# Moving the opening of attention in between the last gate blocks of the projections

## The chip, the core and the metric

The kernel runs on one core of a Trainium2 chip. The metric is the device time of one execution in microseconds. Three runs of the kernel before gave 1424.99 us as median, between 1424.39 and 1425.21.

## What is computed

One decoder layer for 2048 tokens of width 1024, all in float32. A normalised input is projected once; the columns of the projection feed two groups of heads and their gates.

```python
h = rms_norm(x, ln_g)
proj = h @ w_in
q_lat, kv_lat, k_rope, g_mla, hq, hf, hi, g_hg = split(proj)
y_mla = mla_group(q_lat, kv_lat, k_rope, ...) * silu(g_mla)   # 8 heads, causal softmax attention
y_hg  = hgrn2_group(hq, hf, hi, ...) * silu(g_hg)             # 4 heads, gated linear recurrence
x = x + concat(y_mla, y_hg) @ w_out
out = rms_norm(x, final_norm_g)
```

In the attention group the queries and keys come from normalised latents of 256 and 128 columns: `q = q_lat_n @ w_q_b`, `k, v = kv_lat_n @ w_kv_b`, with a rotary part beside them.

## The kernel before

Every product is made of three fp32r matmuls (`mm3`, lines 67 to 70): high by high, high by low, low by high. "Split" means that ScalarE writes the rounded high part (`hi`, line 702) and VectorE the rest (`lo`, line 703); on the `pool=True` path GpSimd does both (lines 699, 700).

The program has three stages. The first (to line 653) makes the projections and the recurrence, 1024 tokens at a time, and writes the latents, the rotary tables and the gates to DRAM (`latq_d`, `latkv_d`, `kpe_d`, `cs_d`, `gate_d`). Its last step is `gates(1, hB)`, line 652: one load of weights and eight blocks of 128 tokens. A block is 24 matmuls of 328 columns into one PSUM bank of the tag `mm`, which has three banks; ScalarE empties it with a SiLU (line 338), and SyncE's queue stores it (line 339). Beside these blocks the last units of the recurrence end: squares (line 513), their sum (515), the scaling (518), a transpose (525), a copy `yt` (527) and its store (528).

The second stage is attention (lines 655 to 1008). It opens with loads of the latents (`load_c`, `load_q`, `load_rope`, `load_cs`, lines 694 to 718) in three slices of the tokens, T0 (0 to 511), T1 (512 to 1023) and T2 (1024 to 2047); with the weights of head 0 (`load_wq`, line 671) and of the keys and values (lines 685 to 692); and with splits of what is loaded. Then come key, query and value of the first 512 tokens (`key`, `query`, `value`), key 1, and the scores of the first two rows of queries (`stage_a(*seq[0], cur)`, line 991). The loop over 64 pairs of head and rows (line 999) merges the scores of the next pair with the transposes and value products of this one. The third stage is the out-projection.

What the first stage holds on the right side of SBUF (pools `raw`, `hg`) is freed by `p1r.close()`, and `lat` of the second stage lies over it; `wk`, `big` and `wk2` lie over the left side after `p1.close()`. A pool that reuses memory waits for all that used it: the first load of attention (line 687) waits for the last store of `yt`.

The lines say in which order work is handed over. A scheduler then sets the order on each engine from its own estimate of the times, and an engine takes its instructions strictly in that order. All loads and stores are issued by SyncE's queue, in its order too.

Of the kernel before, what the change touches and what calls it, by code (L numbers as in the profile page):

```python
# [10 lines left out]
F32 = mybir.dt.float32  # L11
F32R = mybir.dt.float32r
# [7 lines left out]
S = 2048  # L20
D = 1024
# [36 lines left out]
def hybrid_kernel(ctx: ExitStack, tc: tile.TileContext, x, positions, ln_g, w_in, q_a_norm_g, w_q_b,  # L58
# [5 lines left out]
    def f32(ap):  # L64
        return ap.bitcast(F32)
# [583 lines left out]
    U = hg_units(1, 1, raws)  # L649
    merge(U[:16], vv + gg)  # L650
    merge(U[16:], lat_kv(1, hB))
    run(gates(1, hB))
    p1r.close()

# [1 line left out]
    p2 = ExitStack()  # L656
    p2r = ExitStack()
    lat = p2r.enter_context(tc.tile_pool(name="lat", bufs=1, side="right"))
    c_hi = lat.tile([128, S], F32R, name="c_hi")
    c_lo = lat.tile([128, S], F32R, name="c_lo")  # L660
    wv_hi = lat.tile([128, HEADS, VD], F32R, name="wv_hi")
# [9 lines left out]
    def load_wq(h):  # L671
# [9 lines left out]
        A.copy(wqh, wf)  # L681
        G.tensor_tensor(wql, wf, f32(wqh), ALU.subtract)
        return wqh, wql

    G.memset(csT[0:64, 0:1024], 1.0)
    wkv = csT[:, 1024:2048].rearrange("p (h n) -> p h n", h=HEADS)
    DMA.dma_start(wkv, w_kv_b.rearrange("p (h n) -> p h n", h=HEADS))
    V.tensor_scalar(out=wkv, in0=wkv, scalar1=gkv, scalar2=None, op0=ALU.mult)
    A.copy(wk_hi, wkv[:, :, 0:NOPE])
    V.tensor_tensor(wk_lo, wkv[:, :, 0:NOPE], f32(wk_hi), ALU.subtract)  # L690
    A.copy(wv_hi, wkv[:, :, NOPE:128])
    V.tensor_tensor(wv_lo, wkv[:, :, NOPE:128], f32(wv_hi), ALU.subtract)
# [31 lines left out]
    load_c(T0)
    wq0 = load_wq(0)
    load_q(T0)
    load_cs(slice(0, 1024))
    load_rope(T0)
    split_c(T0)
    split_q(T0)  # L730
    split_rope(T0)
    load_c(T1)
    load_q(T1)
    load_rope(T3)
    G.memset(csT[0:64, 1024:2048], 1.0)
    load_cs(T2)
    load_c(T2)
    load_q(T2)
    p1.close()
    wk = p2.enter_context(tc.tile_pool(name="wk", bufs=2, side="left"))  # L740
    big = p2.enter_context(tc.tile_pool(name="big", bufs=1, side="left"))
    wk2 = p2.enter_context(tc.tile_pool(name="wk2", bufs=2, side="left"))
    k_hi1 = big.tile([128, S], F32R, name="k_hi1")
    k_lo1 = big.tile([128, S], F32R, name="k_lo1")
    k_hi, k_lo = (k_hi0, k_hi1), (k_lo0, k_lo1)

    heads = [None] * HEADS

    stash = {}

    def prep(h):
        """Items that make head h's gate, weights, v, k and q (by 512 tokens)."""
        hd = {"k": (k_hi[h % 2], k_lo[h % 2]), "q": [None] * NCHK}
        heads[h] = hd

        def start():
            if h % 2 == 0:
                stash["k"] = wk.tile([64, S], F32, tag="ks", bufs=1, name="ks")
            if h % VG == 0:
                stash["v"] = wk.tile([128, NBLK, VG - 1, VD], F32, tag="vs", bufs=1, name="vs")  # L760
            hd["gate"] = wk2.tile([128, NBLK, VD], F32, tag="gate", name="gate")
            DMA.dma_start(hd["gate"], gate_d[:, h * VD:(h + 1) * VD].rearrange("(b p) n -> p b n", p=128))
            hd["wq"] = wq0 if h == 0 else load_wq(h)
            hd["v"] = wk.tile([128, NBLK, 2, VD], F32R, tag="vp", name="vp")
            if h == 1:
                DMA.dma_start(f32(k_hi1[64:128]), f32(k_hi0[64:128]))
                DMA.dma_start(f32(k_lo1[64:128]), f32(k_lo0[64:128]))

        def value(b4):
# [18 lines left out]

        def key(c):
            kh, kl = hd["k"]  # L790
            ks = stash["k"]
            sl = slice(c * 512, (c + 1) * 512)
            if h % 2 == 0:
                p = bank("b", 1)
                mm3(p, wk_hi[:, h:h + 2].rearrange("p a b -> p (a b)"), wk_lo[:, h:h + 2].rearrange("p a b -> p (a b)"),
                    c_hi[:, sl], c_lo[:, sl], True, True)
                A.copy(kh[0:64, sl], p[0:64])
                V.tensor_tensor(kl[0:64, sl], p[0:64], f32(kh[0:64, sl]), ALU.subtract)
                A.copy(ks[:, sl], p[64:128])
            else:  # L800
                A.copy(kh[0:64, sl], ks[:, sl])
                G.tensor_tensor(kl[0:64, sl], ks[:, sl], f32(kh[0:64, sl]), ALU.subtract)

        def query(c):
            wqh, wql = hd["wq"]
            sl = slice(c * 512, (c + 1) * 512)
            p = mmb()
            for k in range(2):
                mm3(p, wqh[:, k], wql[:, k], q_hi[:, k, sl], q_lo[:, k, sl], k == 0, k == 1)
            qf = wk.tile([128, 512], F32, tag="qf", bufs=1, name="qf")  # L810
            V.tensor_tensor(qf, p, csT[:, sl], ALU.mult)
            qh = wk.tile([128, 512], F32R, tag="qh", bufs=2, name="qh")
            ql = wk.tile([128, 512], F32R, tag="ql", bufs=2, name="ql")
            A.copy(qh, qf)
            (V if h == 0 and c < 2 else G).tensor_tensor(ql, qf, f32(qh), ALU.subtract)  # L815
            hd["q"][c] = (qh, ql)

        its = {"start": start}
        for c in range(NCHK):
            its["k", c] = lambda c=c: key(c)  # L820
            its["v", c] = lambda c=c: value(c)
            its["q", c] = lambda c=c: query(c)
        return its
# [6 lines left out]
        return list(zip(o, w))  # L830

    def stage_a(h, j, ctx_):
        """Scores, negated, with their minimum, then exp: two rows of 128 queries."""
        hd = heads[h]
        items = []
        ctx_["ri"] = [None, None]
# [2 lines left out]
        def score(i, kc):  # L839
# [4 lines left out]
            nk = (qb + 1) * 128  # L844
            chunks = key_chunks(nk)
            if kc == 0:
                ctx_["rows"][i] = wk2.tile([128, S], F32, tag="sn", bufs=4, name="sn")
                ctx_["mx"] = small.tile([128, 5], F32, tag="mx", name="mx")
            sn, mx = ctx_["rows"][i], ctx_["mx"]
            k0, w = chunks[kc]  # L850
# [131 lines left out]
            parts[h][key_]()  # L982
        return do

    for key_ in ("start", ("k", 0), ("q", 0), ("v", 0)):
        parts[0][key_]()
    cur = {}
    av_all = bank("a", 1, (128, 2, 256))
    split_c(T1)
    parts[0]["k", 1]()  # L990
    run(stage_a(*seq[0], cur))
    split_q(T1)
    for i in range(3):
        split_rope(slice(512 + 512 * i, 1024 + 512 * i), pool=True)
    for i in range(2):
        split_c(slice(1024 + 512 * i, 1536 + 512 * i))
    for i in range(2):
        split_q(slice(1024 + 512 * i, 1536 + 512 * i))
# [12 lines left out]
    p3 = ExitStack()  # L1011
    op = p3.enter_context(tc.tile_pool(name="op", bufs=2, side="right"))
    fng = wk.tile([128, D], F32, tag="ks", bufs=1, name="ks")
    DMA.dma_start(fng, final_norm_g.rearrange("(o n) -> o n", o=1).broadcast_to([128, D]))
    for b in range(NBLK):
        c, r0 = b // 4, b * 128
# [67 lines left out]
```

## Time and profile before

| what | value |
|---|---|
| median of three runs | 1424.99 us |
| span of the profiled execution | 1424.0 us |
| TensorE matmul busy | 1395.9 us, 98% of the span |
| VectorE, ScalarE, GpSimd busy | 954.6, 878.6, 464.3 us |
| stretch in question, from the third gate block to full pace in attention | 681.6 to 727.0 us |

The profiled execution's span stands 1.0 us under the median; what lies around the span is in that. The page shows TensorE busy nearly everywhere, with one slice in the middle at 8 tenths instead of 9. That slice holds the passage from projections to attention. In it the time is not TensorE's work but what TensorE waits for, so the rows of that stretch have to be read engine by engine.

### The profile page before, as it was taken

How to read it: one execution, taken by the hardware profiler on the slowest of the kernel's cores; microseconds unless marked ns; L12 is line 12 of the kernel's file. 1: busy time of each engine (PE TensorE's matmuls, PEld its weight loads, DVE VectorE, ACT ScalarE, POOL GpSimd, SP SyncE). 2: the span in 40 equal slices, each digit the busy share in tenths (PEclk: the TensorE clock that was granted, in tenths of full speed). 3: DMA queues.
4: the chain of work that ended last, by engine and by line, in shares of the span. 5: the costliest groups of instructions: out<-in, count | busy, mean ns of one | idle time of the engine just before them, and what ended most of it. 6: DMA issues, size and time to landing. Idle time of an engine off the chain costs nothing.

```text
span 1424.0 us, 25891 instructions
## 1 busy us (share of the span) xinstructions
PE 1395.9 (98%) x9314; PEld 1271.8 (89%) x9314; DVE 954.6 (67%) x2433; ACT 878.6 (62%) x1796; POOL 464.3 (33%) x635
## 2 busy tenths in 40 slices
PE   8999999999999999999989999999999999999998
PEld 7899879989889988999879999999999998888887
DVE  6547855595645746658389889897889888744333
ACT  6565575456672647345387788778877888732232
POOL 3123613083121522227262425233433425411010
PEclk9999999999999999999989999999999999999999
DMA  6211211214221112111640110000010103244342
GB/s 185 75 48 46 75 52 31 70 38 157 64 60 35 45 60 74 45 42 36 165 106 9 28 23 13 22 15 20 15 27 9 25 24 100 79 137 148 133 148 104
DMA packets 96351, 92.10 MB, mean 65 GB/s; under 512 B 31072, under 2 KB 84576, under 8 KB 96096
## 3 DMA queue, kind: packets, MB, share of 16 engines
q1 hardware_dynamic: 96224, 90.46, 21.7%
q8 instruction: 73, 1.20, 0.4%
q14 instruction: 54, 0.44, 0.1%
HBM read 64.22 MB, written 25.17 MB: 63 GB/s over the span
## 4 chain that ended last, share of the span: by engine, by line
PE 86%; DVE 5%; ACT 3%; POOL 2%; DMA 2%; issue 2%; SPq 0%; POOLq 0%; DVEq 0%; ACTq 0%
PE ps_mm L68 14%; PE ps_mm L69 14%; PE ps_mm L70 14%; PE ps_tp L902 8%; PE ps_a L921 5%; PE ps_a L920 4%; PE ps_mm L854 4%; PE ps_mm L855 4%; PE ps_mm L856 4%; PE ps_b L68 2%; PE ps_b L70 2%; PE ps_b L69 2%; PE ps_b L459 1%; PE ps_a L459 1%; POOL dd L441 1%
## 5 line engine op out<-in xcount | busy, mean ns | idle before, releaser
L68 PE MATMUL ps_mm<-w,hh 128*128 128x256 f32 (+3 forms) x896 | 270.2, 302 | 0.0
L69 PE MATMUL ps_mm<-w,hh 128*128 128x256 f32 (+3 forms) x896 | 265.3, 296 | 0.0
L70 PE MATMUL ps_mm<-w,hl 128*128 128x256 f32 (+3 forms) x896 | 264.2, 295 | 0.0
L906 DVE TENSOR_TENSOR pl<-ps_tp,ph 128x512 fp32r<-128x512 f32 (+1 forms) x288 | 184.4, 655 | 32.9 <-ACT ph L905 32.3
L905 ACT CAST ph<-ps_tp 128x512 fp32r<-128x512 f32 (+1 forms) x288 | 154.1, 565 | 61.5 <-PE ps_tp L902 47.3
L68 PEld LDWEIGHTS ps_mm<-w,hh 128*128 128x128 f32 x896 | 171.4, 191 | 1.0 <-ACT kr L234 0.3
L69 PEld LDWEIGHTS ps_mm<-w,hh 128*128 128x128 f32 x896 | 171.2, 191 | 0.4
L70 PEld LDWEIGHTS ps_mm<-w,hl 128*128 128x128 f32 x896 | 170.6, 190 | 0.1
L902 PE MATMUL ps_tp<-ident,sn 128*128 128x128 f32 x1088 | 168.1, 274 | 0.6 <-ACT sn L868 0.5
L868 ACT ACTIVATE sn<-sn,mx 128x128 f32<-128x128 f32 (+15 forms) x128 | 154.6, 1208 | 21.5 <-DVE mx L863 21.0
L920 PE MATMUL ps_a<-ph,vp 128*128 128x256 f32 x576 | 155.5, 290 | 0.0
L921 PE MATMUL ps_a<-pl,vp 128*128 128x256 f32 x576 | 147.3, 289 | 0.3 <-DVE pl L906 0.2
L441 POOL TENSOR_TENSOR dd<-G 128x512 f32<-128x512 f32 x80 | 92.9, 1166 | 144.0 <-DVE qd L454 109.3
L902 PEld LDWEIGHTS ps_tp<-ident,sn 128*128 128x128 f32 x1088 | 126.9, 140 | 8.5 <-ACT sn L868 1.1
L854 PE MATMUL ps_mm<-k_hi,qh 128*128 128x512 f32 (+3 forms) x320 | 131.1, 410 | 0.3 <-DVE sn L859 0.2
L859 DVE TENSOR_SCALAR_CACHE_REDUCE sn<-ps_mm,mx 128x512 f32<-128x512 f32 (+3 forms) x192 | 111.5, 581 | 10.0 <-PE ps_mm L856 8.3
L856 PE MATMUL ps_mm<-k_hi,ql 128*128 128x512 f32 (+3 forms) x320 | 116.7, 365 | 1.2 <-DVE ql L815 1.2
L855 PE MATMUL ps_mm<-k_lo,qh 128*128 128x512 f32 (+3 forms) x320 | 116.4, 364 | 0.0
L203 DVE SCALAR_TENSOR_TENSOR w<-wr,lng,w 128x256 fp32r<-128x256 f32 (+3 forms) x168 | 88.4, 568 | 39.3 <-ACT w L202 39.3
L921 PEld LDWEIGHTS ps_a<-pl,vp 128*128 128x128 f32 x576 | 109.1, 189 | 6.1 <-DVE pl L906 1.4
L920 PEld LDWEIGHTS ps_a<-ph,vp 128*128 128x128 f32 x576 | 109.0, 189 | 5.8 <-ACT ph L905 0.4
L887 POOL TENSOR_SCALAR gp<-gate,ri 128x64 f32<-128x64 f32 x128 | 56.3, 443 | 174.1 <-DVE ri L870 158.4
(275 smaller groups left out, 3355.3 us busy)
## 6 DMA issues: line engine op xcount, KB each, us to landing
wr<-in_w_in SPq DMA_DIRECT2D x68, 256.0 KB
yl<-y_d SPq DMA_DIRECT2D x16, 512.0 KB
vp<-in_x SPq DMA_DIRECT2D x16, 512.0 KB
out<-sn SPq DMA_DIRECT2D x15, 512.0 KB
xt<-in_x SPq DMA_DIRECT2D x8, 512.0 KB
y_d<-yt SPq DMA_DIRECT2D x16, 256.0 KB
gate<-gate_d SPq DMA_DIRECT2D x8, 512.0 KB
y_d<-oa SPq DMA_DIRECT2D x64, 64.0 KB
```

What stands on the lines that cost most here:

```text
L68: PE.matmul(ps, l_hi, r_hi, start=start, stop=False)
L69: PE.matmul(ps, l_hi, r_lo, start=False, stop=False)
L70: PE.matmul(ps, l_lo, r_hi, start=False, stop=stop)
L854: PE.matmul(p[:, :w], qh[:, qs], kh[:, ks], start=True, stop=False)
L855: PE.matmul(p[:, :w], qh[:, qs], kl[:, ks], start=False, stop=False)
L856: PE.matmul(p[:, :w], ql[:, qs], kh[:, ks], start=False, stop=True)
L868: A.activation(sn[:, :nk], sn[:, :nk], AF.Exp, bias=mx[:, kc:kc + 1], scale=-1.0, accum_out=rs)
L902: PE.transpose(tp[:, o:o + 128], prow[i][:, (kb + u) * 128:(kb + u + 1) * 128], ident)
L905: A.copy(ph[:, :w], tp[:, :w])
L906: V.tensor_tensor(pl[:, :w], tp[:, :w], f32(ph[:, :w]), ALU.subtract)
L920: PE.matmul(dst, vv, ph[:, rng], start=st_, stop=False)
L921: PE.matmul(dst, vv, pl[:, rng], start=False, stop=en)
```

## The change

The gates of the last half are no longer run to their end. Only their weights are loaded first (`ga[:1]`); the eight blocks are then merged evenly with a list of items: the loads of attention, its weights, the splits, key 0, query 0, key 1, the scores of the first pair and the remaining splits. Value 0 and the load of the gate stay behind the blocks. Pools of the second stage get `reuse_waits="tile"`, so that a tile waits only for the tiles that it lies over. The scratch of dynamic DMAs is cut to 2048 bytes, and three tags (`ks`, `qf`, `qh`/`ql`) and two small rows (`sn0`) move to a new pool `qk` on the right side.

```diff
-    run(gates(1, hB))
+    ga = gates(1, hB)
+    run(ga[:1])
     p1r.close()
...
+    qk = p2q.enter_context(tc.tile_pool(name="qk", bufs=1, side="right", reuse_waits="tile"))
+    lat = p2r.enter_context(tc.tile_pool(name="lat", bufs=1, side="right", reuse_waits="tile"))
...
-    for key_ in ("start", ("k", 0), ("q", 0), ("v", 0)):
-        parts[0][key_]()
+    def first_loads():
+        load_c(T0)
+        parts[0]["start_k"]()
+        load_q(T0)
+        load_cs(slice(0, 1024))
+        load_rope(T0)
+    def more_loads():
+        load_c(T1)
+        load_q(T1)
+        load_rope(T3)
+        G.memset(csT[0:64, 1024:2048], 1.0)
+        load_cs(T2)
+        load_c(T2)
+        load_q(T2)
+    def opening():
+        split_rope(T0)
+        parts[0]["k", 0]()
+        parts[0]["q", 0]()
+    items = [first_loads, weights, lambda: (split_c(T0), split_q(T0)), more_loads, opening,
+             lambda: split_c(T1), parts[0]["k", 1]] + stage_a(*seq[0], cur)
+    items += [lambda: split_q(T1)] + [lambda i=i: split_rope(thirds(i), pool=True) for i in range(3)]
+    items += [lambda i=i: split_c(thirds(i + 1)) for i in range(2)]
+    items += [lambda i=i: split_q(thirds(i + 1)) for i in range(2)]
+    merge(ga[1:], items)
+    p1.close()
...
+    parts[0]["start"]()
+    parts[0]["v", 0]()
-    nc = bacc.Bacc("TRN2", target_bir_lowering=False, num_devices=1)
+    nc = bacc.Bacc("TRN2", target_bir_lowering=False, num_devices=1, dynamic_dma_scratch_size=2048)
```

`weights` is the old code of lines 685 to 692, and `start_k` takes the tile `ks` and `load_wq` out of `start`. The order on all engines is the same before the third gate block, and nearly the same from the second pair of rows on. Three places show what lies between.

TensorE, before, at the third gate block (`ps_mm<-w,hh`, 328 columns; `ps_tp<-ident,sq` are the transposes of the recurrence's last two units):

```order
L68 MATMUL ps_mm<-w,hh 128x328
L69 MATMUL ps_mm<-w,hh 128x328
L525 MATMUL ps_tp<-ident,sq 128x128 x2
L503 MATMUL ps_tp<-S_7489,qt 128x128
L502 MATMUL ps_tp<-rv,at_103 128x128
L503 MATMUL ps_tp<-S_7493,qt 128x128
L525 MATMUL ps_tp<-ident,sq 128x128 x2
L316 MATMUL ps_tp<-ident,lk 128x128 x4
```

The same place in the changed kernel:

```order
L525 MATMUL ps_tp<-ident,sq 128x128 x4
L503 MATMUL ps_tp<-S_7489,qt 128x128
L502 MATMUL ps_tp<-rv,at_103 128x128
L503 MATMUL ps_tp<-S_7493,qt 128x128
L316 MATMUL ps_tp<-ident,lk 128x128 x4
L525 MATMUL ps_tp<-ident,sq 128x128 x4
L68 MATMUL ps_mm<-q_hi,wqh 128x512
L68 MATMUL ps_mm<-w,hh 128x328
L69 MATMUL ps_mm<-w,hh 128x328
```

Both groups of transposes, and the first matmul of query 0 (`q_hi,wqh`), now stand ahead of the third gate block; before, the second group stood behind the fourth block, and query 0 behind all eight.

SyncE's queue before, from the last store of `yt` on:

```order
L528 DMA y_d_72<-yt 128x512
L687 DMA csT<-in_w_kv_b 128x1024
L695 DMA c_lo<-latkv_d 128x512
L673 DMA wf<-in_w_q_b 128x2x96
L339 DMA gate_d<-gt 128x328
L709 DMA q_lo<-latq_d 128x2x512
L715 DMA csT<-cs_d 64x1024
L718 DMA k_lo_7857<-kpe_d 64x512
L695 DMA c_lo<-latkv_d 128x512
L709 DMA q_lo<-latq_d 128x2x512
L718 DMA k_lo_7857<-kpe_d 64x1536
L695 DMA c_lo<-latkv_d 128x1024
```

In the changed kernel, from the same store on:

```order
L528 DMA y_d_72<-yt 128x512
L689 DMA c_lo<-latkv_d 128x512
L676 DMA wf<-in_w_q_b 128x2x96
L703 DMA q_lo<-latq_d 128x2x512
L709 DMA csT<-cs_d 64x1024
L712 DMA k_lo_7636<-kpe_d 64x512
L970 DMA csT<-in_w_kv_b 128x1024
L689 DMA c_lo<-latkv_d 128x512
L703 DMA q_lo<-latq_d 128x2x512
L712 DMA k_lo_7636<-kpe_d 64x1536
L689 DMA c_lo<-latkv_d 128x1024
L703 DMA q_lo<-latq_d 128x2x1024
```

The loads still stand behind that store. The first is now `c_lo`, the weights of keys and values come sixth, and the gate stores have moved behind all loads.

ScalarE before, from the split of the second slice of `q` on (`gt<-ps_mm` empties a gate block, `ks<-ps_b` the bank of key 0, which key 1 takes next):

```order
L702 CAST q_hi<-q_lo 128x2x512
L338 ACTIVATE gt<-ps_mm 128x328
L797 CAST k_hi_7856<-ps_b 64x512
L702 CAST c_hi<-c_lo 128x512 x2
L799 COPY ks<-ps_b 64x512
L781 CAST vp<-ps_mm 128x2x64
L801 CAST k_hi_7904<-ks 64x512
L781 CAST vp<-ps_mm 128x2x64
L814 CAST qh<-qf 128x512
L797 CAST k_hi_7856<-ps_b 64x512
L783 COPY vs<-ps_mm 128x384 x2
L702 CAST q_hi<-q_lo 128x2x512 x2
```

In the changed kernel, from the same split on:

```order
L696 CAST q_hi<-q_lo 128x2x512
L696 CAST c_hi<-c_lo 128x512 x2
L338 ACTIVATE gt<-ps_mm 128x328
L774 CAST k_hi_7635<-ps_b 64x512
L791 CAST qh<-qf 128x512
L696 CAST q_hi<-q_lo 128x2x512 x2
L776 COPY ks<-ps_b 64x512
L338 ACTIVATE gt<-ps_mm 128x328
L774 CAST k_hi_7635<-ps_b 64x512
L848 ACT_TABLE_LOAD
L848 ACTIVATE sn_7813,rs<-sn_7813,mx 128x128
L848 ACTIVATE sn_7824,rs<-sn_7824,mx 128x256
```

The copy `ks` of key 0 now stands behind the two splits of the last and largest load of `q_lo`; before, it stood ahead of them. The gate that it follows is the third here and the eighth before. On TensorE key 1 (three matmuls into `ps_b`), which waits for `ks`, now stands between the fourth and the fifth gate block, so the last four blocks stand behind it.

## Rows read from the trace of the kernel before

**Rows 1.** The page's busy times: engine, busy us, share of the span, instructions.
```profile
PE 1395.9 (98%) x9314; PEld 1271.8 (89%) x9314; DVE 954.6 (67%) x2433; ACT 878.6 (62%) x1796; POOL 464.3 (33%) x635
```

**Rows 2.** Stretches: length, busy by engine, granted TensorE clock, DMA share, GB/s.
```profile
650.00:652.00 2.00, 1.85 (x11) 1.72 (x11) 2.00 (x3) 0.72 (x2) 2.00 (x3) 0.68 0.00 0
654.00:656.00 2.00, 2.00 (x18) 2.00 (x17) 2.00 (x7) 1.48 (x5) 2.00 (x4) 0.96 0.09 27
708.00:713.00 5.00, 1.15 (x8) 0.77 (x6) 1.82 (x2) 2.23 (x4) 2.52 (x4) 0.92 1.02 261
713.00:718.00 5.00, 2.36 (x6) 1.53 (x7) 4.73 (x7) 4.70 (x11) 4.85 (x4) 0.50 1.07 317
718.00:723.00 5.00, 4.45 (x13) 3.46 (x14) 4.95 (x16) 4.85 (x9) 3.24 (x5) 0.50 0.83 170
681.60:727.00 45.40, 38.37 (x223) 35.24 (x222) 21.69 (x48) 23.37 (x46) 17.87 (x21) 0.85 0.79 198
```

**Rows 3.** TensorE's waits, 681.6 to 728 us: who waits for whom, total, times, longest.
```profile
PE ps_b L68 <- ACT ks L799: 3.3, 1, 3.3
PE ps_mm L68 <- ACT gt L338: 2.0, 1, 2.0
```

**Rows 4.** Timeline of TensorE: start, length, line, operation, tiles, shapes, [idle before <-releaser].
```profile
681.63 0.31 PE L68 MATMUL ps_mm<-w,hh 128*128 128x328 f32 x1
...
682.83 0.38 PE L525 MATMUL ps_tp<-ident,sq 128*128 128x128 f32 x2
...
684.29 0.40 PE L70 MATMUL ps_mm<-w,hl 128*128 128x328 f32 x1
...
705.24 0.39 PE L68 MATMUL ps_b<-c_hi,wk_hi 128*128 128x512 f32 x1
...
707.30 0.28 PE L68 MATMUL ps_mm<-wv_hi,c_hi 128*128 128x256 f32 x1
...
707.89 0.28 PE L70 MATMUL ps_mm<-wv_hi,c_lo 128*128 128x256 f32 x1
...
727.01 0.42 PE L854 MATMUL ps_mm<-k_hi,qh 128*128 128x384 f32 x1
```

**Rows 5.** Timeline of ScalarE, 684 to 721 us.
```profile
684.19 0.60 ACT L513 ACTIVATE sq<-ps_tp 128x512 f32<-128x512 f32 x1 [1.91 <-PE ps_tp L525]
...
691.38 0.69 ACT L527 ACTIVATE yt<-ps_tp,hng 128x512 f32<-128x512 f32 x1 [0.19 <-PE ps_tp L525]
...
701.50 0.41 ACT L681 CAST wqh<-wf 128x256 fp32r<-128x256 f32 x1
703.38 1.05 ACT L702 CAST q_hi<-q_lo 128x1024 fp32r<-128x1024 f32 x1 [1.47 <-DMA q_lo<-latq_d]
...
712.62 1.14 ACT L702 CAST c_hi<-c_lo 128x512 fp32r<-128x512 f32 x2 [2.06 <-DMA c_lo<-latkv_d]
...
717.33 2.00 ACT L702 CAST q_hi<-q_lo 128x1024 fp32r<-128x1024 f32 x2
...
719.66 0.58 ACT L799 COPY ks<-ps_b 64x512 f32<-64x512 f32 x1
720.26 1.28 ACT L868 ACT_TABLE_LOAD   x1
```

**Rows 6.** Timeline of VectorE, two groups.
```profile
686.92 1.12 DVE L518 SCALAR_TENSOR_TENSOR sq<-ps_tp,rop,rg 128x128 f32<-128x128 f32 x4 [1.41 <-POOL rop L76]
...
699.67 0.45 DVE L675 TENSOR_SCALAR wf<-wf,gq 128x96 f32<-128x96 f32 x2 [0.51 <-DMA wf<-in_w_q_b]
```

**Rows 7.** Timeline of SyncE's queue: the instant of each issue.
```profile
692.10 0.32 SPq L528 DMA_DIRECT2D y_d<-yt  x1
694.24 0.33 SPq L687 DMA_DIRECT2D csT<-in_w_kv_b  x1
...
695.09 0.43 SPq L673 DMA_DIRECT2D wf<-in_w_q_b  x1
...
696.08 0.43 SPq L709 DMA_DIRECT2D q_lo<-latq_d  x1
```

More of the change, by code (lines that the diff above doesn't have):

```diff
@@ L657, in hybrid_kernel @@
     p2r = ExitStack()
-    lat = p2r.enter_context(tc.tile_pool(name="lat", bufs=1, side="right"))
+    p2q = ExitStack()
+    qk = p2q.enter_context(tc.tile_pool(name="qk", bufs=1, side="right", reuse_waits="tile"))
+    lat = p2r.enter_context(tc.tile_pool(name="lat", bufs=1, side="right", reuse_waits="tile"))
     c_hi = lat.tile([128, S], F32R, name="c_hi")
@@ L683, in load_wq @@
         return wqh, wql
[L685 to L692, printed above, removed]
     def load_c(sl):
@@ L723, in hybrid_kernel @@
     T0, T1, T2, T3 = slice(0, 512), slice(512, 1024), slice(1024, 2048), slice(512, 2048)
[L724 to L745, printed above, removed]
     heads = [None] * HEADS
@@ L751, in prep, with start_k @@
     def prep(h):
-        hd = {"k": (k_hi[h % 2], k_lo[h % 2]), "q": [None] * NCHK}
+        hd = {"k": (k_hi1, k_lo1) if h % 2 else (k_hi0, k_lo0), "q": [None] * NCHK}
         heads[h] = hd
+        def start_k():
+            if h % 2 == 0:
+                stash["k"] = qk.tile([64, S], F32, tag="ks", bufs=1, name="ks")
+            hd["wq"] = load_wq(h)
         def start():
-            if h % 2 == 0:
-                stash["k"] = wk.tile([64, S], F32, tag="ks", bufs=1, name="ks")
+            if h:
+                start_k()
             if h % VG == 0:
@@ L761, in start @@
             hd["gate"] = wk2.tile([128, NBLK, VD], F32, tag="gate", name="gate")
-            DMA.dma_start(hd["gate"], gate_d[:, h * VD:(h + 1) * VD].rearrange("(b p) n -> p b n", p=128))
-            hd["wq"] = wq0 if h == 0 else load_wq(h)
+            for b0, b1 in ((0, 8), (8, NBLK)) if h == 0 else ((0, NBLK),):
+                DMA.dma_start(hd["gate"][:, b0:b1], gate_d[b0 * 128:b1 * 128, h * VD:(h + 1) * VD]
+                              .rearrange("(b p) n -> p b n", p=128))
             hd["v"] = wk.tile([128, NBLK, 2, VD], F32R, tag="vp", name="vp")
@@ L809, in query @@
                 mm3(p, wqh[:, k], wql[:, k], q_hi[:, k, sl], q_lo[:, k, sl], k == 0, k == 1)
-            qf = wk.tile([128, 512], F32, tag="qf", bufs=1, name="qf")
+            qf = qk.tile([128, 512], F32, tag="qf", bufs=1, name="qf")
             V.tensor_tensor(qf, p, csT[:, sl], ALU.mult)
-            qh = wk.tile([128, 512], F32R, tag="qh", bufs=2, name="qh")
-            ql = wk.tile([128, 512], F32R, tag="ql", bufs=2, name="ql")
+            qh = qk.tile([128, 512], F32R, tag="qh", bufs=2, name="qh")
+            ql = qk.tile([128, 512], F32R, tag="ql", bufs=2, name="ql")
             A.copy(qh, qf)
@@ L816, in query @@
             hd["q"][c] = (qh, ql)
-        its = {"start": start}
+        its = {"start": start, "start_k": start_k}
         for c in range(NCHK):
@@ L846, in score @@
             if kc == 0:
-                ctx_["rows"][i] = wk2.tile([128, S], F32, tag="sn", bufs=4, name="sn")
+                if h == 0 and j == 0:
+                    ctx_["rows"][i] = qk.tile([128, 256], F32, tag="sn0", bufs=2, name="sn0")
+                else:
+                    ctx_["rows"][i] = wk2.tile([128, S], F32, tag="sn", bufs=4, name="sn")
                 ctx_["mx"] = small.tile([128, 5], F32, tag="mx", name="mx")
@@ L983, in part, with weights @@
         return do
-    for key_ in ("start", ("k", 0), ("q", 0), ("v", 0)):
-        parts[0][key_]()
     cur = {}
-    av_all = bank("a", 1, (128, 2, 256))
[L989 to L998, printed above, removed]
+    def weights():
+        G.memset(csT[0:64, 0:1024], 1.0)
+        wkv = csT[:, 1024:2048].rearrange("p (h n) -> p h n", h=HEADS)
+        DMA.dma_start(wkv, w_kv_b.rearrange("p (h n) -> p h n", h=HEADS))
+        V.tensor_scalar(out=wkv, in0=wkv, scalar1=gkv, scalar2=None, op0=ALU.mult)
+        A.copy(wk_hi, wkv[:, :, 0:NOPE])
+        V.tensor_tensor(wk_lo, wkv[:, :, 0:NOPE], f32(wk_hi), ALU.subtract)
+        A.copy(wv_hi, wkv[:, :, NOPE:128])
+        V.tensor_tensor(wv_lo, wkv[:, :, NOPE:128], f32(wv_hi), ALU.subtract)
@@ new lines, in first_loads, with thirds @@
+    def first_loads():
[12 more added lines that the diff above has]
+        load_q(T2)
+    def thirds(n):
+        return slice(512 + 512 * n, 1024 + 512 * n)
+    def opening():
+        split_rope(T0)
+        parts[0]["k", 0]()
+        parts[0]["q", 0]()
@@ new lines, in hybrid_kernel @@
+    items = [first_loads, weights, lambda: (split_c(T0), split_q(T0)), more_loads, opening,
[5 more added lines that the diff above has]
+    p1.close()
+    wk = p2.enter_context(tc.tile_pool(name="wk", bufs=2, side="left", reuse_waits="tile"))
@@ L999, in hybrid_kernel @@
+    big = p2.enter_context(tc.tile_pool(name="big", bufs=1, side="left", reuse_waits="tile"))
+    wk2 = p2.enter_context(tc.tile_pool(name="wk2", bufs=2, side="left", reuse_waits="tile"))
+    k_hi1 = big.tile([128, S], F32R, name="k_hi1")
+    k_lo1 = big.tile([128, S], F32R, name="k_lo1")
+    parts[0]["start"]()
+    parts[0]["v", 0]()
+    av_all = bank("a", 1, (128, 2, 256))
     for n, (h, j) in enumerate(seq):
@@ L1012, in hybrid_kernel @@
     op = p3.enter_context(tc.tile_pool(name="op", bufs=2, side="right"))
-    fng = wk.tile([128, D], F32, tag="ks", bufs=1, name="ks")
+    fng = qk.tile([128, D], F32, tag="ks", bufs=1, name="ks")
     DMA.dma_start(fng, final_norm_g.rearrange("(o n) -> o n", o=1).broadcast_to([128, D]))
@@ L1054, in hybrid_kernel @@
     p2r.close()
+    p2q.close()
     p2.close()
```

## The prediction

> **What bounds the kernel now.** I read the page's busy times first: TensorE is busy for 98% of the span [rows 1], so only the places where it waits or runs slowly can give anything back. The list of stretches shows one such place, 681.6 to 727.0 us: 38.4 us busy in 45.4, at a mean clock of 0.85 [rows 2]. TensorE's waits there name two stops, 2.0 us for a gate block's emptying and 3.3 us for `ks` [rows 3]; in the stretches the clock then falls to 0.50, which is 1.2 GHz, and stays there for some 11 us [rows 2]. The timeline gives a start and an end for the comparison. The third gate block begins at 681.63. The second group of scores of 384 columns, of the pair after the opening, begins at 727.01 [rows 4]; from there on the order is nearly the same in both kernels. Between these two instants the change has to win or lose.
>
> What the stretch holds at full clock, from the spacing of starts [rows 4]: a gate matmul costs 0.15 us (eight from 681.63 to 682.83), so a block of 24 costs 3.6 and the six left 21.6. A 512-column matmul costs 0.23 (nine from 705.24 to 707.30), a 256-column one 0.12 (five from 707.30 to 707.89). With 11 small matmuls of the recurrence (1.46 us, 682.83 to 684.29), four more transposes (0.5) and the opening of attention, that is some 32 to 33 us. So about 12 to 13 us of the 45.4 are idle or slow, and this is all that the change can win.
>
> **Step 1, the recurrence's end.** In the new order TensorE does the 11 small matmuls right after the second gate block: 681.63 + 1.46 = 683.1 us. Then come the transposes of the last unit. They need the chain square, sum, power, scaling, which takes from 684.19 [rows 5] to 686.92 + 1.12 = 688.04 [rows 6], 3.85 us. The square can start 1.2 us earlier, since eight gate matmuls no longer stand before it: 682.99, and the chain ends at 686.8. Before, the third and fourth gate blocks covered it. Now TensorE is idle from 683.1 to about 686.3 and done with the transposes at 687.0.
>
> **Step 2, the loads.** They stand behind the last store of `yt` on SyncE's queue. From the transposes' end to that store it took 0.8 us (691.29, two pieces before ScalarE's 691.38 [rows 5], to 692.10 [rows 7]), so the store is issued at 687.8. Before, the first load then waited until 694.24 for the store to land [rows 7]; waits by tile take these 2 us away, and the first load goes out at 688.2 instead of 694.24. This is the gain of the change, 6 us on the loads.
>
> When they land I take from two rows of before, counting what was issued up to each. `q_lo` T0 was there at 703.38, 9.14 us after the first issue, with 1.58 MB; `c_lo` T2 at 712.62, 18.38 us after it, with 3.67 MB [rows 5, 7]. That is 2.2 us plus 4.4 us per MB. Changed: `wf` (0.36 MB in all) lands at 688.2 + 3.8 = 692.0; or at 693.2, by its own 4.6 us from issue (695.09 [rows 7]) to use (699.67 [rows 6]). From its arrival to the end of `wqh` it took 701.91 - 699.67 = 2.24 us [rows 5, 6], hence 694.2 to 695.5. `q_lo` T0 (0.88 MB) lands at 694.3. Its split takes 1.05 [rows 5]. `q_hi` is therefore ready between 695.4 and 696.5; I take 696.0. The lower end, with all landing 2 us after issue as the store did, is 694.0; the upper, with `q_lo`'s own 7.3 us from issue to use, 697.5.
>
> TensorE takes its instructions in order, and the first matmul of query 0 stands ahead of the third gate block. **It is idle from 687.0 to 696.0, 9.0 us,** with six gate blocks queued behind that one matmul that need nothing of these loads.
>
> **Step 3, blocks three and four.** From 696.0: 48 gate matmuls (7.2) and nine of 512 columns (2.1), 9.3 us at full clock. After a stop the clock is low. In one case it was back within some 3.4 us of dense work (0.68 in 650 to 652, 0.96 in 654 to 656), in the other only after some 11 us of broken work [rows 2]. Half clock costs half of its duration: 1.7 or 5.7 us. Here the work is dense, so 1.7: they end at 707.0.
>
> **Step 4, key 1.** It waits for `ks`, which on ScalarE stands behind the splits of the last `q_lo`, 4.55 MB after the first issue: 688.2 + 22.3 = 710.5. Two splits take 2.00 and `ks` 0.58 [rows 5]: 713.1. The six small score matmuls (1.0 us) fit in before; they need `c_lo` T2 (705.8) and the steps behind it, which are done by 709. Key 1 takes 0.7, so the fifth gate block starts at 713.8: **5 us more of idling.** If the data are early, this wait is nothing.
>
> **Step 5, the rest.** Four gate blocks 14.4, to 728.2; a second dip of the clock 1.0 (between 0 and 1.7). Then to the compared matmul: 24 matmuls of value 0 (2.9), query 1 (1.4), two groups of scores (1.2), five transposes and four small products (0.7), 6.2 in all, of which 0.4 stands behind the compared instant in the kernel before. Waits for ScalarE's emptying there 0.5 (0 to 2.5; two more table loads of 1.28 [rows 5] lie beside the gate blocks and cost nothing, since a bank is needed only a block later). Sum: 728.2 + 1.0 + 6.2 - 0.4 + 0.5 = 735.5, against 727.01: 8.5 us later. Everything after keeps its length; the scratch size and the split gate load are put at nothing, the latter hidden by some 7 us of TensorE's work. The profiled span becomes 1432.5, and with the 1.0 us by which the median exceeds it, **1433.5 us.**
>
> Bounds of the sum: restart at 694.0 and no wait at key 1, no second dip, no late wait: -0.5 us. Restart at 697.5, the long dip twice, loads a tenth slower, late waits of 2.5: +16.
>
> **Rivals.** *Loads faster* (B). The stretch 713 to 718 moved 317 GB/s [rows 2]. With 2.06 us and 3.15 us per MB, `q_hi` is ready at 694.7, blocks three and four end at 705.7, `ks` at 707.2 and key 1 at 707.9, 5.9 us sooner: 1427.6. For it: no gate stores among these loads. Against: 261 and 170 GB/s in the stretches beside it. The Trainium skill, "DMA: Bandwidth & Descriptors", sections on one DMA's anatomy and on measured bandwidth, gives about 2 us of fixed cost and 341 GB/s for a load of 1 MB; an estimate by that page would put key 1 6.5 us sooner, at 1427.0. The trace agrees on the fixed cost (2.06 us for the store), not on the rate.
>
> *Faster* (C). If `q_hi` were there when TensorE reaches query 0, the 9.0 us and the wait at key 1 vanish and no dip follows: 687.0 + 9.3 + 1.7 + 14.4 + 5.8 = 718.2, 8.8 us sooner than before: 1416. It decides at 687.0 us: `q_lo` would have to be issued by about 680. Against it, the loads stand behind a store that can't be issued before 687.8.
>
> *The clock stays low* (D). The dips last as long as after 712, some 12 us each: 4 more in the second, hidden partly in the first: 1438.5. For it: the work is broken by two stops. Against: each is followed by two to four dense blocks.
>
> **How the numbers follow.** The forecast (A) 60%, B 17%, C 5%, D 18%. About 0.2%, 2.8 us, is what a measurement of this kernel can tell from no change. C is faster. B lies at that limit, so 0.12 of its share goes to no change and the rest to slower. Faster 0.05, same 0.12, slower 0.83. The range 1426.5 to 1440 holds A, D and most of B.
>
> **What would show it.** In the changed profile: one wait of TensorE of 8 to 10 us at the first `q_hi,wqh` matmul, released by the split of `q_hi`, just before the third gate block; some 3 us before the last transposes of `sq`; 2 to 6 us at `ps_b` of key 1, released by `ks`; the clock at 0.50 after the first; loads issued from 688. Wrong would be a third gate block that starts by 690, or a matmul of 384 columns like that of 727.01 before 727. If the first wait is there and the time is still no longer, steps 3 to 5 are mis-sized.

## The result and the profile after

The changed kernel takes 1433.84 us (median of four, three of them between 1432.49 and 1434.52), 1.0056 times the kernel before [1.0042, 1.0070]. A second measurement gave 1434.96 us and 1.0067 [1.0054, 1.0079]. Forecast were 1433.5 us and a range of 1426.5 to 1440.

The fourth, the profiled one, was disturbed (its span was 4851.9 us); without it the median is 1433.16 us, and all rows below come from the second measurement, of the same kernel.

The busy times [rows 1 for before] hardly move: TensorE does the same work with the same number of instructions, in a span that is 9.1 us longer than the 1424.0 us of before.

```profile
PE 1396.9 (97%) x9314; PEld 1274.0 (89%) x9314; DVE 954.9 (67%) x2433; ACT 881.3 (61%) x1798; POOL 464.8 (32%) x635
```

TensorE's waits from 675 to 760 us (who waits for whom, total, times, longest) answer to [rows 3]. Three long stops stand where two stood: 14.4 us together, against 5.3 of those two and another 1.8 in two short ones behind them.

```profile
PE ps_mm L68 <- ACT q_hi L696: 9.5, 1, 9.5
PE ps_tp L525 <- DVE sq L518: 2.9, 1, 2.9
PE ps_b L68 <- ACT ks L776: 2.0, 1, 2.0
```

TensorE's timeline, for [rows 4]: the end of the second gate block (the row of 682.50 begins what follows it), the three stops in the order of time, the fifth gate block, and the compared matmul.

```profile
682.50 0.60 PE L525 MATMUL ps_tp<-ident,sq 128*128 128x128 f32 x4
...
687.09 1.16 PE L525 MATMUL ps_tp<-ident,sq 128*128 128x128 f32 x4 [2.88 <-DVE sq L518]
697.71 0.80 PE L68 MATMUL ps_mm<-q_hi,wqh 128*128 128x512 f32 x1 [9.46 <-ACT q_hi L696]
...
712.67 0.50 PE L68 MATMUL ps_b<-c_hi,wk_hi 128*128 128x512 f32 x1 [2.00 <-ACT ks L776]
...
713.48 0.31 PE L68 MATMUL ps_mm<-w,hh 128*128 128x328 f32 x1
...
736.47 0.34 PE L834 MATMUL ps_mm<-k_hi,qh 128*128 128x384 f32 x1
```

In this execution the second gate block ends at 682.50 instead of 681.63. The 0.87 us stand there already at 236 us, far ahead of the change; between the kernels below, whose order up to there is the same, such offsets differ by some 2 us. Taking the 0.87 off, the compared matmul stands at 735.60 against 727.01 [rows 4]: 8.6 us later. That is nearly all of the 9.1 us of the spans, so the loss lies in this one stretch, as forecast.

The stretches (length, busy by engine, granted clock, DMA share, GB/s) answer to [rows 2], the first being that of the comparison:

```profile
682.50:736.47 53.97, 39.30 (x228) 37.12 (x225) 21.47 (x47) 26.43 (x49) 17.37 (x18) 0.81 0.57 154
683.60:687.00 3.40, 0.61 (x6) 0.37 (x4) 1.09 (x3) 1.30 (x3) 1.64 (x3) 0.95 0.55 204
687.00:690.00 3.00, 1.16 (x4) 0.73 (x4) 0.72 (x3) 0.69 (x1) 0.45 (x1) 0.50 0.04 15
690.00:697.70 7.70, 0.00 (x0) 0.00 (x0) 1.05 (x4) 2.07 (x3) 1.55 (x3) 0.50 0.99 240
697.70:702.00 4.30, 4.29 (x15) 4.19 (x16) 4.06 (x6) 2.28 (x4) 0.00 (x0) 0.50 1.07 315
702.00:704.00 2.00, 2.00 (x10) 2.00 (x9) 0.50 (x1) 1.04 (x1) 0.00 (x0) 0.57 0.96 265
704.00:706.00 2.00, 2.00 (x12) 1.70 (x11) 1.24 (x2) 0.67 (x2) 1.55 (x2) 1.00 1.03 408
...
710.00:712.60 2.60, 0.67 (x6) 0.47 (x5) 2.30 (x3) 2.55 (x3) 2.20 (x3) 1.00 0.02 7
712.60:714.00 1.40, 1.33 (x7) 1.19 (x8) 1.40 (x2) 0.79 (x3) 1.40 (x2) 0.99 0.02 7
714.00:716.00 2.00, 2.00 (x9) 2.00 (x8) 1.51 (x8) 1.97 (x5) 1.47 (x2) 0.50 0.21 79
716.00:718.00 2.00, 2.00 (x10) 2.00 (x10) 0.33 (x2) 1.96 (x5) 0.00 (x0) 0.65 0.00 0
```

The clock is at 0.50 (1.2 GHz) from 687 to about 703.7: after the restart at 697.7 that is 6 us of work at half speed, 3 us lost. It falls again at 714, until about 717.2; the four blocks from 713.48 to the value products at 729.41 take 15.9 us instead of 14.4, so another 1.5 us go.

Still, the stops and not the clock make the loss. TensorE is idle for 14.7 us of the first stretch (53.97 - 39.30), and for 7.0 of the same stretch before (45.40 - 38.37 [rows 2]): 7.6 of the 8.6 us. Counted as the part of the busy time that the granted clock is short of full, the low clock takes 5.3 us here and took some 4.8 before, by [rows 2] from 708 to 723 and this row of the kernel before:

```profile
723.00:727.00 4.00, 4.00 (x22) 3.51 (x21) 2.68 (x10) 2.32 (x8) 2.23 (x4) 0.65 1.12 201
```

What released TensorE stands on ScalarE and SyncE, for [rows 5, 7]. ScalarE first: `q_hi` waits 0.90 us for its load, and `ks` stands behind the splits of the last `q_lo`, for which ScalarE waited 1.95 us.

```profile
695.32 0.40 ACT L684 CAST wqh<-wf 128x256 fp32r<-128x256 f32 x1 [1.19 <-POOL wf L681]
696.62 1.04 ACT L696 CAST q_hi<-q_lo 128x1024 fp32r<-128x1024 f32 x1 [0.90 <-DMA q_lo<-latq_d]
...
710.02 1.99 ACT L696 CAST q_hi<-q_lo 128x1024 fp32r<-128x1024 f32 x2 [1.95 <-DMA q_lo<-latq_d]
712.04 0.58 ACT L776 COPY ks<-ps_b 64x512 f32<-64x512 f32 x1
```

SyncE's queue: the store of `yt`, and the first load 0.45 us behind it, where [rows 7] had 2.1 us between the two.

```profile
689.05 0.32 SPq L528 DMA_DIRECT2D y_d<-yt  x1
689.50 0.34 SPq L689 DMA_DIRECT2D c_lo<-latkv_d  x1
```

### The profile page after: what moved, and what is told of

It is laid out like the page before. It is cut to its first block, busy times and chain, and to the rows that moved or that the text cites. A ratio compares the mean times of both kernels' runs of the same rounds, so it can differ in the third digit from the quotient of the medians.

```text
span 4851.9 us, 25876 instructions
## 1 busy us (share of the span) xinstructions
PE 4833.6 (100%) x9314; PEld 3552.6 (73%) x9314; DVE 972.6 (20%) x2433; ACT 916.9 (19%) x1798; POOL 445.4 (9%) x635
## 4 chain that ended last, share of the span: by engine, by line
PE 99%; issue 0%; DMA 0%; ACT 0%; DVE 0%; POOL 0%; SPq 0%; POOLq 0%; ACTq 0%
PE ps_mm L68 17%; PE ps_mm L70 17%; PE ps_mm L69 17%; PE ps_tp L882 9%; PE ps_mm L834 5%; PE ps_mm L835 5%; PE ps_a L900 5%; PE ps_a L901 5%; PE ps_mm L836 5%; PE ps_b L459 2%; PE ps_a L459 2%; PE ps_b L69 2%; PE ps_b L70 2%; PE ps_b L68 2%; PE ps_tp L502 1%; PE ps_tp L178 1%
## 5 line engine op out<-in xcount | busy, mean ns | idle before, releaser
L68 PE MATMUL ps_mm<-w,hh 128*128 128x256 f32 (+3 forms) x896 | 657.2, 734 | 0.0
L69 PE MATMUL ps_mm<-w,hh 128*128 128x256 f32 (+3 forms) x896 | 644.1, 719 | 0.0
L70 PE MATMUL ps_mm<-w,hl 128*128 128x256 f32 (+3 forms) x896 | 644.0, 719 | 0.0
L882 PE MATMUL ps_tp<-ident,sn 128*128 128x128 f32 x1088 | 522.0, 681 | 0.0
L70 PEld LDWEIGHTS ps_mm<-w,hl 128*128 128x128 f32 x896 | 478.0, 533 | 29.7 <-issue 10.9
L69 PEld LDWEIGHTS ps_mm<-w,hh 128*128 128x128 f32 x896 | 477.2, 533 | 29.7 <-issue 10.7
L68 PEld LDWEIGHTS ps_mm<-w,hh 128*128 128x128 f32 x896 | 471.4, 526 | 29.8 <-issue 11.0
L900 PE MATMUL ps_a<-ph,vp 128*128 128x256 f32 x576 | 408.5, 709 | 0.0
L901 PE MATMUL ps_a<-pl,vp 128*128 128x256 f32 x576 | 385.1, 678 | 0.0
L834 PE MATMUL ps_mm<-k_hi,qh 128*128 128x512 f32 (+3 forms) x320 | 357.1, 1117 | 0.0
L68 PE MATMUL ps_mm<-hh,w 128*128 128x512 f32 x256 | 282.5, 1107 | 0.0
L70 PE MATMUL ps_mm<-hh,w 128*128 128x512 f32 x256 | 281.6, 1106 | 0.0
L69 PE MATMUL ps_mm<-hl,w 128*128 128x512 f32 x256 | 281.5, 1101 | 0.0
```

The costliest lines, as they stand in the source:

```text
L68: PE.matmul(ps, l_hi, r_hi, start=start, stop=False)
L69: PE.matmul(ps, l_hi, r_lo, start=False, stop=False)
L70: PE.matmul(ps, l_lo, r_hi, start=False, stop=stop)
L834: PE.matmul(p[:, :w], qh[:, qs], kh[:, ks], start=True, stop=False)
L882: PE.transpose(tp[:, o:o + 128], prow[i][:, (kb + u) * 128:(kb + u + 1) * 128], ident)
L900: PE.matmul(dst, vv, ph[:, rng], start=st_, stop=False)
```

## The experiments

Eleven kernels were run. The theory (A): TensorE's order is fixed, query 0 and key 1 stand ahead of gate blocks that need no load, and the loads come late. R1: the moved tiles and the tile-wise waits cost. R2: ScalarE (table loads, late emptying) costs. D: the low clock sets the price. All ratios are to the kernel before, measured on the same chip. To compare instants of several kernels, they are counted below from the first `ps_tp<-ident,sq` row of TensorE, which is 682.50 in the changed kernel ("after sq"). Where the code runs blocks ahead, eight matmuls of the third gate block (1.2 us) stand ahead of that row; comparisons with such a kernel count from the end of the second block.

**The changed kernel again.** No edit.

> The changed kernel again, for a trace in which TensorE runs as usual. Theory A (two stops of TensorE, because its instructions stand in a fixed order and loads come too late for it): some 1433.5 us; one wait of 8 to 10 us at the first query matmul, just before the third gate block, one of about 3 us before the last transposes of the recurrence, one of 2 to 6 us at key 1, and the clock at half after the first. Rival R1 (the pools that wait tile by tile and the tiles that moved cost the time): the waits are on stores and loads of reused tiles, scattered through attention. Rival R2 (ScalarE, with two more table loads and late emptying of gate banks): TensorE's waits in the stretch are on the SiLU of gate blocks.

Measured: 1434.96 us; its rows are those above.

**All blocks ahead, the rest of the change kept.**

```diff
-    merge(ga[1:], items)
+    run(ga[1:] + items)
```

> Only the pools, the scratch and the moved tiles of the change; the eight gate blocks are all handed over ahead of the opening of attention, as before. A: no stop between gate blocks, first load 2 us sooner than before since it does not wait for the last store to land, 1420 to 1424 us. R1: the loss stays, 1430 us or more. R2: near the kernel before, 1425.

Measured: 1424.58 us, 0.9995 [0.9986, 1.0004]. With the new pools, tags, split loads and scratch but the gate blocks ahead as before, the time is that of before: R1 falls, and the whole loss comes from the merge. Nor is there a gain to tell from noise, where 1420 to 1424 was expected, though the loads no longer wait for the store: a stop for `qh` has come where 3.3 us for `ks` stood.

```profile
PE ps_mm L834 <- ACT qh L791: 3.8, 1, 3.8
```

**Six of eight blocks ahead.**

```diff
-    merge(ga[1:], items)
+    run(items[:1] + ga[1:7])
+    merge(ga[7:], items[1:])
```

> First loads handed over ahead, then six gate blocks, and the rest of the opening merged with the last two blocks only. A: the third to sixth gate blocks cover most of the time of the loads; a stop of 0 to 3 us at the first query matmul in place of 9, none or a short one at key 1, 1415 to 1421 us. R1: 1430 or more, since the pools are those of the change. R2: between, 1425 to 1430, since silu and exp still alternate.

Measured: 1422.89 us, 0.9985 [0.9976, 0.9994]: 12 us under the changed kernel, some 2 us under the kernel before and the fastest of all, but not as low as expected. Its waits of TensorE show one stop at query 0 left and smaller ones behind (three more, of 0.7 us and less, are left out here).

```profile
PE ps_mm L68 <- ACT q_hi L696: 2.4, 1, 2.4
PE ps_mm L834 <- ACT qh L791: 1.2, 1, 1.2
PE ps_mm L834 <- ACT vs L760: 0.9, 1, 0.9
```

SyncE's queue in the same kernel shows why the first is left:

```profile
692.70 0.32 SPq L528 DMA_DIRECT2D y_d<-yt  x1
693.44 0.31 SPq L689 DMA_DIRECT2D c_lo<-latkv_d  x1
```

Blocks three and four now run ahead of the last transposes of `sq`. They cover the 2.9 us stop there, but they put off the store of `yt` and with it the first load, to 11.2 us behind the second gate block (693.44 - 682.23) instead of 7.0 (689.50 - 682.50). The expectation counted the cover and does not mention the later loads.

**The last splits on GpSimd.**

```diff
-    items += [lambda i=i: split_q(thirds(i + 1)) for i in range(2)]
+    items += [lambda i=i: split_q(thirds(i + 1), pool=True) for i in range(2)]
```

> The changed kernel with the last two splits of q given to GpSimd, so that on ScalarE the copy that key 1 waits for no longer stands behind the last and largest load. TensorE's order is that of the changed kernel. A: the stop at the first query matmul stays at 8 to 10 us, that at key 1 falls from 2 to 6 us to 2 or less, 1428 to 1431 us. If the stop at key 1 costs nothing (the loads are early, rival B of the prediction): as the changed kernel, 1433 to 1434. R1 and R2: the same as the changed kernel.

Measured: 1430.58 us, 1.0039 [1.0026, 1.0052]. The row for `ks` is gone, the other two stops stay (9.8 and 2.9), a wait of 0.6 us has come at the scores, and no dip of the clock follows at 714:

```profile
704.00:733.00 29.00, 28.07 (x184) 26.85 (x183) 11.62 (x33) 16.33 (x34) 18.53 (x17) 1.00 0.56 147
```

The second stop was worth about 4 us by the times, its 2.0 us and the half clock behind it (1.5) among them; in the trace the compared matmul comes 3.4 us sooner (50.6 us after sq instead of 54.0).

**The stop at query 0 filled with idle work.**

```diff
+            if last_unit:
+                wm = stash["wm"] = const.tile([128, 128], F32R, name="wm")
+                A.copy(wm, tp[:, 0:128])
...
+            if h == 0 and c == 0:
+                for i in range(36):
+                    PE.matmul(p, stash["wm"], hB[0]["hi"][:, i % 4], start=True, stop=True)
```

> The changed kernel, with 36 matmuls of 512 columns put ahead of the first matmul of query 0 (8.3 us at 0.23 each, results unused; they read a small copy of the last transposes). They fill the stop at query 0 with idle work and keep the clock up; nothing else moves. Theory A (fixed order, late loads): query 0 still can't start before q_hi is there, so the third gate block starts where it did. The dip of the clock (0.50 for some 6 us after the stop, about 3 us lost) goes, blocks three and four end some 3 us sooner, but key 1 then waits for ks as before, since the last q_lo lands when it lands: the stop at key 1 grows from 2.0 to 4 to 5 us and the time stays within 1 us of the changed kernel, 1433 to 1435.5. Rival D (the clock sets the price): 3 us or more come back, 1430.5 or less.

Measured: 1435.30 us (1430.76 to 1437.41), 1.0069 [1.0055, 1.0084], no change against the kernel without the matmuls (1.0067). In its waits of TensorE the stop at query 0 is gone, that at `sq` (2.9 us) is as before, and others have come:

```profile
PE ps_b L68 <- ACT ks L780: 2.5, 1, 2.5
PE ps_mm L842 <- DVE k_lo L779: 1.1, 1, 1.1
PE ps_mm L791 <- ACT wm L534: 1.0, 1, 1.0
PE ps_b L68 <- ACT wk_hi L979: 0.9, 1, 0.9
PE ps_mm L841 <- ACT k_hi L778: 0.3, 1, 0.3
```

The granted clock was back at 1.00 by 692 and stayed there until about 711. The growth expected at key 1 alone (to 4 or 5 us) was spread: 0.9 at key 0, 1.4 at the scores, 2.5 at key 1. So the 3 us or more that D wanted back did not come.

But this was no clean removal of the dip. The first of the 36 matmuls ran at half clock (0.50 in 688 to 690), so that they took longer than 8.3 us, and the third gate block began 0.8 us after `q_hi` was written (695.63 + 1.05 = 696.68):

```profile
687.81 9.82 PE L791 MATMUL ps_mm<-hh,wm 128*128 128x512 f32 x36 [0.98 <-ACT wm L534]
697.47 0.32 PE L68 MATMUL ps_mm<-w,hh 128*128 128x328 f32 x1
695.63 1.05 ACT L702 CAST q_hi<-q_lo 128x1024 fp32r<-128x1024 f32 x1 [1.28 <-DMA q_lo<-latq_d]
```

The scores behind block four began 27.2 us after sq, where the changed kernel has 27.3, and the last `q_lo` came 1.8 us later (29.3 against 27.5), though it was issued at about the same time (14.4 and 14.1). Why it came later stays open, and the times of this kernel spread over 6.7 us. That a wait for a load takes whatever the dip gives back is therefore not shown by this run alone.

**Both.** The matmuls and the splits on GpSimd.

> The same 36 matmuls, and the splits of the last two slices of q_lo on GpSimd, so that ks no longer stands behind them. Compared with the kernel that had only the splits moved (ratio 1.0039 to the kernel before). Theory A: with key 1 free, the 3 us of the clock's dip do come back, less what key 0 and key 1 then wait for their own c_lo: 1.5 to 3 us, ratio 1.0018 to 1.0028, 1427.5 to 1429. If the dip costs nothing by itself (its price is only that of the stop): as without the matmuls, 1430.5.

Measured: 1431.63 us, 1.0052 [1.0038, 1.0067]: nothing came back, where 1.5 to 3 us were expected. Key 1 starts 28.46 us after sq, and 28.48 with the splits alone. What ends last is now the scores' chain on ScalarE (idle time before an instruction, and its releaser, in brackets):

```profile
706.29 1.14 ACT L702 CAST c_hi<-c_lo 128x512 fp32r<-128x512 f32 x2 [1.78 <-DMA c_lo<-latkv_d]
707.34 0.61 ACT L798 CAST qh<-qf 128x512 fp32r<-128x512 f32 x1
707.86 0.57 ACT L778 CAST k_hi<-ps_b 64x512 fp32r<-64x512 f32 x1
```

`qh` and `k_hi`, which the scores need, stand behind the split of the third slice of `c_lo`, and ScalarE waits 1.78 us for that load. A load ends the chain again, by another engine's order, so a faster TensorE gains nothing here. That load, too, came later than with the splits alone (its split began 24.2 us after sq instead of 23.5), which the run doesn't explain.

**Waits by the whole freed memory.**

```diff
-    lat = p2r.enter_context(tc.tile_pool(name="lat", bufs=1, side="right", reuse_waits="tile"))
+    lat = p2r.enter_context(tc.tile_pool(name="lat", bufs=1, side="right"))
```

and the same in the pools `qk`, `wk`, `big` and `wk2`.

> The changed kernel, with pools that wait for the whole of the freed memory, as before the change (tile-wise waits taken out; the order of the work stays). Theory A: the first load then waits again for the last store of yt to land, 2.0 us; everything that hangs on the loads, query 0 and key 1, moves by up to 2 us: 1435 to 1437, the stop at query 0 11 to 12 us instead of 9.5. Rival R1 (tile-wise waits are what costs): 1425 to 1430.

Measured: 1437.33 us, 1.0086 [1.0072, 1.0100]. R1 falls again: tile-wise waits are not what costs. But the place that the expectation named was wrong. The first load went out at 8.55 us after sq instead of 7.0, and the stop at query 0 stayed at 9.6, since the split of the first `q_lo` began 4.7 us after its issue (695.12 - 690.45) instead of 6.2 (696.62 - 690.38). The loss came behind key 1: a longer stretch at the low clock and a wait of 1.2 us at the first value products. Why the load took less time was not tried, and the intervals of the two kernels overlap.

**Query 0 from other data.**

```diff
+                if h == 0 and c == 0:
+                    xh, xl = hB[0]["hi"], hB[0]["lo"]
+                    mm3(p, xh[:, 2 + k, 0:128], xl[:, 2 + k, 0:128], xh[:, k], xl[:, k], k == 0, k == 1)
+                    continue
```

> Query 0 of head 0 for the first 512 tokens reads the normalised input instead of the loaded latents and weights (same six matmuls, other data, so that its values are others). The six then stand ahead of the third gate block and wait for nothing; the order behind them has blocks three and four ahead of the recurrence's last transposes, so the loads go out some 4 us later, at about 693. Theory A: the stop does not vanish, it moves to the next instruction that needs a load, key 0 (c_hi, wk_hi) behind block four: 9 to 13 us there, but once and not twice, since ks now stands ahead of the last splits: 1424 to 1430. Rival R3 (query 0's own chain of weights and split is the price, not the loads in general): no stop over 4 us, 1416 to 1422.

Measured: 1435.23 us, 1.0074 [1.0061, 1.0086]. The stop moved to key 0, as A said, but it is 14.3 us long, beyond the 9 to 13 expected, and the time is as long as with two stops, where 1424 to 1430 was expected.

```profile
PE ps_b L68 <- ACT wk_hi L976: 14.3, 1, 14.3
PE ps_mm L68 <- DVE mx L847: 2.0, 1, 2.0
PE ps_mm L838 <- ACT k_hi L774: 0.7, 1, 0.7
```

Query 0's own chain (R3) is not the price: with it gone, the next instruction that needs a load stops the same queue. The weights of the keys are the sixth load, and the first went out 12.2 us behind the second gate block in this order (693.55 - 681.38) instead of 7.0, behind blocks three and four and the store of `yt`. Since the loads moved too, the time does not weigh the chain by itself; what speaks against R3 is the stop of 14.3 us, where R3 wanted none over 4.

**Four blocks ahead.**

```diff
+    run(items[:1] + ga[1:5])
+    merge(ga[5:], items[1:])
```

> Four gate blocks run ahead of the merged list, and the other four are merged with the items behind the loads. On TensorE query 0 still stands ahead of the third gate block; key 1 now stands in the fifth block's successor, one block and a half later than in the changed kernel. Theory A (what counts is which work stands behind the first instructions that need a load): the stop at query 0 stays, 9 to 10 us; the stop at key 1 goes, since ks is written by then; 1429 to 1432, like the kernel with the splits moved to GpSimd. Rival E (the number of blocks run first in the code is what counts, each block taking 3.6 us off the stop): 1424 to 1428.

Measured: 1428.89 us, 1.0032 [1.0020, 1.0044]. The expectation had TensorE's order wrong: blocks three to five stand ahead of query 0. The stop there is 6.2 us, and `ks` is waited for no longer. With six blocks ahead it is 2.4: `q_hi` was there 17.93 and 17.81 us after sq in the two, and one more block (3.6 us by [rows 4]) took 3.7 us off. So E's price per block is right, and its time (1424 to 1428) too low: other waits, 2.6 us at the scores and 1.7 for the emptying of a bank, stand in what follows.

**Six and seven blocks, weights and q first, splits on GpSimd.**

```diff
     def first_loads():
-        load_c(T0)
         parts[0]["start_k"]()
         load_q(T0)
+        load_c(T0)
...
+    items += [lambda i=i: split_q(thirds(i + 1), pool=True) for i in range(2)]
+    run(items[:1] + ga[1:7])
+    merge(ga[7:], items[1:])
```

and `ga[1:8]`, `ga[8:]` for seven.

> Six gate blocks run ahead, as in the kernel that took 1422.89; the weights and the first slice of q are loaded ahead of the first slice of c; the last splits of q on GpSimd. Theory A: q_hi is ready some 0.5 to 1 us sooner, so the stop of 2.4 us at query 0 shrinks to 1.4 to 2; the rest stays: 1421 to 1423. If ScalarE's queue is what ends the later waits (1.2 us at qh), moving 2 us of splits off it gives another microsecond; if GpSimd comes late with them, query 1 waits instead, 1423 to 1425.

> The same with seven gate blocks ahead. Theory A: TensorE reaches query 0 some 3.6 us later than with six, when q_hi is there: no stop at query 0; but only one block is left for the chain from query 0 to the scores, and what the eighth block covered stands bare (with all eight ahead the wait at qh was 3.8 us): 1420 to 1424.

Measured: 1427.90 us (1423.42 to 1429.97), 1.0011 [1.0002, 1.0021], and 1427.93 us, 1.0012 [1.0000, 1.0025]. Both lie above what was expected (1421 to 1423 and 1420 to 1424). With six, the stop at query 0 fell to 1.0 us, more than expected, and the kernel still lost some 4 us against the plain six blocks (0.9985). With seven there is none, but key 0 waits 2.8 us for the weights of the keys, and half a microsecond more. The stretch from the start of the third gate block to the 61st value product (`ps_a<-ph,vp`), behind which the distance of the two kernels stays the same, of the six blocks with the edits:

```profile
681.77:792.97 111.20, 103.73 (x648) 91.75 (x647) 74.95 (x213) 72.53 (x150) 45.42 (x59) 0.97 0.33 91
```

And of the plain six blocks:

```profile
682.23:786.96 104.73, 98.66 (x648) 90.74 (x647) 74.51 (x215) 74.28 (x152) 42.90 (x55) 0.98 0.36 97
```

For the same 648 matmuls TensorE was idle for 1.4 us more and busy for 5.1 more. The low clock explains some 1.7 of these: it was 0.84 in 710 to 720 and 0.87 in 720 to 730, where the plain six blocks had 1.00, and in turn 0.94 against 0.83 in 700 to 710. Which of the two edits brings it was not separated, nor where the rest goes; GpSimd takes 1.0 us for the high and 2.4 us for the low part of a slice, where ScalarE takes 1.0 for the high part and VectorE writes the low one.

## Why the prediction was right

The direction, the place, the three stops and what released them came as forecast. Of the sizes, the first dip, the landing of the last load and the way behind the blocks were off; that the sum came out within 0.1 us all the same is luck. All instants are on the clock of before (0.87 us taken off).

**Step 1**, the recurrence's end: 3.2 us forecast, 2.9 measured, by the chain named.

**Step 2**, the loads: the store went out at 688.2 (forecast 687.8) and the first load at 688.6 (688.2). `wqh` was written by 694.9, within the forecast's 694.2 to 695.5. The first `q_lo` was split from 695.75, 1.4 us later than its landing by the forecast, and query 0 began at 696.8 instead of 696.0. The stop is 9.5 us instead of 9.0.

**Step 3** failed in its size. The clock was back after 6 us of work from the restart, not after 3.4, and took 3 us instead of 1.7; the scores behind block four began at 708.95, where the forecast had the blocks done at 707.0. The other case that the forecast read, some 11 us, was too short: 45.4 us at a mean clock of 0.85 [rows 2] are 13.6 us at the low level.

**Step 4** failed in its size the other way. The last `q_lo` was there at 709.15 instead of 710.5, and key 1 started at 711.8 instead of 713.1. Since TensorE also came later, only 2.0 us of the 5 were seen as a stop. The two terms are no sum of separate costs: when key 1 starts is set by the load, since TensorE waited 2.0 us for `ks` there, so up to 2 us less ahead of it would have gained nothing. The runs with the filled stop gained nothing either, but there the loads came later too. The forecast took key 1's start from the load and so got nearly the right instant, though blocks three and four ended 2 us late.

**Step 5**: the fifth block began at 712.6 (forecast 713.8), the second dip took 1.5 us (1.0), and the way from value 0 to the compared matmul was 7.1 us (6.3). So -1.2, +0.5 and +0.8 make the 735.6 against 735.5: three errors that cancel.

**The rivals.** B, faster loads, did not come: the last `q_lo`, 4.55 MB after the first issue, was there 20.5 us after it. With the 2.06 us that the prediction takes for the store (the whole time of 0.26 MB) that is 4.1 us per MB, nearer to the forecast's 4.4 than to B's 3.15. The estimate by the Trainium skill, "DMA: Bandwidth & Descriptors", measured bandwidth (341 GB/s for a load of 1 MB, there issued from GpSimd), is not borne out by these loads queued by SyncE: 1 MB in 4.1 us is some 245 GB/s. C needed `q_hi` at 687; it was there ten microseconds later. D wanted dips of some 12 us each; TensorE worked 6 us at the low level behind the first stop and 3.2 behind the second. R2 (table loads, late emptying) found no such wait in the changed kernel, where the table loads lie beside TensorE's work between the blocks; with four blocks ahead it did, in the 1.7 us for a gate bank, whose emptying stands right behind a table load of 1.28 us on ScalarE.

## What to carry to other kernels

Where queues run in order, work merged "evenly" by the source is a bet on when data land: an instruction that needs a load must stand behind enough work that needs none, on TensorE and also on the engine that prepares its operand. Count the cover from the last event that the load itself waits for; a block moved ahead may cover a wait and put off that event, as the store of `yt` did here. And where a load ends a wait, time saved ahead of that wait is lost in it, up to its length (here the 2.0 us at key 1); look for the wait that ends last before paying for the savings.

## What was not expected of the hardware

In the changed kernel the clock did not fall at the second stop's beginning: the stop began near 710.7 and ended at 712.67, and the granted clock was 0.99 until 714.0, when TensorE had been at work for 1.3 us. A stop of 2 us thus cost 1.5 us more after its end. The clock was back after 6 us of work behind the first stop, and after some 3 us at the low level behind the second.

The rate of the loads is uneven at nearly the same share of busy DMA engines: 240 GB/s at 0.99 in 690.0 to 697.7, 408 GB/s at 1.03 in 704 to 706. And a load's own time moved by 1.5 us between kernels whose queue was nearly the same (6.2 and at most 4.7 us for the first `q_lo`, changed kernel and whole-memory waits), so a forecast of one landing was good to no more than that here.
